# First stage of a two-block transformer kernel: which engine splits weights and doubles a rotation table

## The chip, the cores and the metric

The kernel runs on one core of a Trainium2 chip. The core has a matrix engine (TensorE, PE in the profile, whose weight loads are shown as PEld), two elementwise engines that this document is about, VectorE (DVE) and GpSimd (POOL), an engine for activation functions and copies (ScalarE, ACT), and SyncE (SP), which here only issues the loads. Each engine runs its own list of instructions strictly in order and waits on semaphores for the others. The metric is the device time of one execution in microseconds (us), lower is better. Three runs of the kernel before gave 973.45, 974.07 and 975.14 us, median 974.07.

## The reference

Two blocks run after each other on 256 tokens of width 1024, in float32. The part that matters here is the first half of the first block:

```
h = layer_norm(concat([meta (16 rows), x (256 rows)]))          # 272 x 1024
p = h @ w_in + b_in                                             # 1024 x 5640
u, q, k, v, o, i, f, g_s5, g_m = split(p)                       # widths 512 512 512 1024 1024 4 4 1024 1024
qk   = silu(causal_depthwise_conv(concat([q, k]), width 4))
s5   : x_t = exp(lambda*dt) x_{t-1} + Bbar u_t (complex);  y_t = Re(C x_t) + D u_t
mlstm: chunked matrix memory over q, k, v, i, f; head norm; times sigmoid(o)
mix  = sigmoid(g_s5) * glu(gelu(s5)) + sigmoid(g_m) * (mlstm @ m_w_out)
h    = layer_norm(alpha*h + mix @ w_o); then a feed-forward part; then the second block:
       attention, gated delta rule, mixture of experts, final norm
```

The complex recurrence of s5 is done as a real scan in a rotating frame: angle tables cos(n*theta) and sin(n*theta) for n = 0..63 turn the input into the frame and the state out of it.

## The kernel before

The float32 products are made of three fast ones: each operand is split into a rounded high part and a low remainder (`whi` and `wlo` for weights, `hTh` and `hTl` for the normalised tokens), and `ws` (L438) issues hi*hi, hi*lo and lo*hi. One slice of `w_in` is 128 columns wide: a 128x1024 tile, 24 matmuls of 272 (later 256) columns. The 45 slices are counted here as w0 to w44: w0 to w3 give u, w4 to w11 q and k, w12 the gates i and f, w13 to w20 v, w21 to w28 o, w29 to w44 the two mix gates.

For each slice `wsplit` (L417) lets ScalarE round the weights into `whi` and lets VectorE, or GpSimd if `eng` says so, subtract to get `wlo`. Both have three buffers, so the split of slice n waits until TensorE is through with slice n-3. `pool_turn` (L604) chose the engine: the first two slices in `ln0` (L594) and the next three (PT = 3) go to GpSimd, then from the 13th turn on every fourth, later every third: 14 of the 45, namely w0, w1, w3, w4, w5, w18, w22, w26, w30, w32, w35, w38, w41 and w44.

A q/k slice ends in one of two PSUM banks. ScalarE empties it into `pre` and `cv_y` (two buffers each), VectorE adds three shifted products to `cv_y` (`conv_silu`, L858), ScalarE takes a tanh (`cv_t`) and VectorE writes `qk`. So TensorE can be at most a few slices ahead of VectorE.

`s5_setup` (L634) makes the tables between these projections: a long run of small VectorE instructions (exponentials, angles, `bd`, `cz`), one Sin on ScalarE (`cs`), and then `double` (L728), six times: from the first 2^k columns of the two tables `rot` it makes the next 2^k by an angle addition of four products, a difference and a sum, each a tensor_tensor over 16 x 2^k elements a partition. 36 instructions in all, on GpSimd. The tables are first read after the v projection has begun, in `s5` (L742), which interleaves with v, o and gate projections: products with `rot` on VectorE, sums on GpSimd (`s5z`, 32 of them), scans on VectorE.

`block1` (L1007) calls these as generators in a fixed order. `ln0` runs in a hand-written order on VectorE, ScalarE and TensorE; from L1027 on a scheduler of the tile framework orders each engine's list from the order of emission and its own cost estimates, so that any edit can reorder the rest of the stage.

Of the kernel before, what the change touches and what calls it, by code (L numbers as in the profile page):

```python
# [11 lines left out]
OP = mybir.AluOpType  # L12
# [58 lines left out]
MS = {mybir.EngineType.DVE, mybir.EngineType.Activation, mybir.EngineType.PE}  # L71
NW0 = 1
NWU = 30
PT = 3
LT = 9
DCE = 1
QB = 3
# [1 line left out]
PV = 3  # L79
ORD0 = "0m1w"  # L80
PW = 4
P0 = 12
PP = [9]
L1A = [2, 2, 2, 2]
ORD = "abcdefmnopyz"
# [7 lines left out]
class K:  # L93
    def __init__(self, ctx, tc, a, out, dbg=None, stop=None):
# [3 lines left out]
        nc = self.nc  # L98
        self.V, self.S, self.G, self.PE, self.SP = nc.vector, nc.scalar, nc.gpsimd, nc.tensor, nc.sync
        self.const = self.pool("const", 1)  # L100
        self.DC = (self.G, self.V)[DCE]
        self.psx = None
# [118 lines left out]
    def setup(self):  # L221
        nc, a, const = self.nc, self.a, self.const
        V, G = self.V, self.G
        self.ones = const.tile([128, 128], F32, name="ones")
        jp = self.ones.bitcast(I32)
        G.iota(jp, pattern=[[1, 128]], base=0, channel_multiplier=-1)
        self.ident = const.tile([128, 128], F32, name="ident")
        self.ts(self.ident, jp, 0.0, OP.is_equal, eng=G)
        self.warm = const.tile([128, 1], F32, name="warm")

    def setup2(self, lp):
        nc, a, const = self.nc, self.a, self.const
        V, G = self.V, self.G
        jp = self.ones.bitcast(I32)
# [265 lines left out]
    def ln0(self):  # L500
# [27 lines left out]
        def chain(x, tag, dg, n=128):  # L528
            v, m, y, t = [lp.tile([128, 1], F32, name=f"r0{j}", tag=f"{tag}{j}")[:n] for j in range(4)]
            self.ts(v, x, 1.0, OP.mult, 1e-5, OP.add)  # L530
            self.ts(m, x, -0.5, OP.mult, -0.5e-5, OP.add)
            yield
            self.ts(y.bitcast(I32), v.bitcast(I32), -0.5, OP.mult, 1597463007.0, OP.add)
            yield
            for _ in range(3):
                self.stt(t, y, m, y, OP.mult, OP.mult)
                yield
                self.stt(y, t, 1.5, y, OP.add, OP.mult)
                yield
            self.ts(dg, self.ident[:n, :n], y, OP.mult)  # L540
            if n == 128:
                V.tensor_copy(self.rs0[:, int(tag[1]):int(tag[1]) + 1], y)

        def run(*gens):
            gens = list(gens)
            while gens:
                gens = [q for q in gens if next(q, 0) is None]

        def centre(x, h, ag):
            for cs in (slice(0, 512), slice(512, 1024)):  # L550
                self.stt(h[:, cs], x[:, cs], ag[:, 0:1], g[:, cs], OP.subtract, OP.mult)
                yield

        def stats(x, st, ag):
            for i in range(2):
                V.bn_stats(st[:, i], x[:, i * 512:(i + 1) * 512])
                yield
            V.bn_aggr(ag, st)
# [8 lines left out]
        def one(f):  # L567
            f()
            yield

        with self.tc.manual_schedule(engines=MS):
            for o, n in ((0, 32), (32, 4)):
                rs = slice(o, o + n)
                self.cpa(self.sel[rs], self.ident[rs, o:o + 4, None].to_broadcast([n, 4, 128]))
            brow = lp.tile([36, 256], F32R, name="brow0")
            self.act(brow, self.sel.bitcast(F32).rearrange("p a b -> p (a b)")[:, :256], AF.Copy, scale=0.0)
            p = self.ps("acc")
            for _ in range(NWU):
                self.tr(p[:, :128], self.ident)
            self.act(self.warm, self.ident[:, 0:1], AF.Tanh)  # L580
            self.act(brow[0:4], br.rearrange("p a b -> p (a b)"), AF.Copy)
            self.act(hs, xm, AF.Copy, accum_out=sm)
            run(stats(xs[0], st[0], ag[0]))
            run(one(lambda: self.tt(brow[32:36], br.rearrange("p a b -> p (a b)"), brow[0:4].bitcast(F32), OP.subtract)),
                chain(ag[0][:, 1:2], "l0", dg[0]), centre(xs[0], self.hres[0], ag[0]),
                self.late(3, one(lambda: self.ts(sm, sm, -1.0 / D, OP.mult))),
                self.late(4, stats(xs[1], st[1], ag[1])))
            self.act(hm, xm, AF.Identity, bias=sm)
            self.act(hs, hm, AF.Square, accum_out=qm)
            self.tt(hm, hm, g[:16], OP.mult, eng=self.G)  # L590
            tn = self.tn(16, self.hres[0], dg[0], self.hT, brow)
            run(chain(ag[1][:, 1:2], "l1", dg[1]), centre(xs[1], self.hres[1], ag[1]),
                one(lambda: self.ts(qm, qm, 1.0 / D, OP.mult)), self.late(3, chain(qm, "l2", dg[2], 16)), self.late(LT, tn))
            self.wsp = [self.wsplit(self.w0[0][:, :, j * 128:(j + 1) * 128], 0, eng=self.G) for j in range(2)]  # L594
            run(self.tn(144, self.hres[1], dg[1], self.hT, brow))
            next(ls)
            run(self.tn(0, hm, dg[2], self.hT, brow))
            self.setup2(lp)
            next(ls)
            wv = self.w0[1]  # L600
            self.wsp += [self.wsplit(wv[:, :, j * 128:(j + 1) * 128], 0) for j in range(NW0)]
        self.ls, self.sl = ls, sl

    def pool_turn(self):  # L604
        self.np += 1
        return self.G if self.np > P0 and self.np % (PW if self.np < PN else PV) == 0 or self.np <= PT else None

# [26 lines left out]
    def s5_setup(self, pool, tmp):  # L634
# [80 lines left out]
        tq = [tmp.tile([128, 16, 32], F32, name=f"tq{i}") for i in range(2)]  # L715
        self.G.memset(self.rot[0][:, :, 0:1], 1.0)
        self.G.memset(self.rot[1][:, :, 0:1], 0.0)
        for k in range(6):
            self.double(self.rot, k, 2 ** k, tq)
        yield  # L720
        for o, v in [(self.BT[i], bd[i].rearrange("p (c a) b -> p c (a b)", c=4)) for i in range(2)] + list(zip(self.CT, czs)):
            p = self.ps("acc")
            for c in range(4):
# [4 lines left out]
    def double(self, src, k, n, tq):  # L728
        C, Sn = src[0][:, :, 0:n], src[1][:, :, 0:n]
        cb = self.cs[:, 0, k, :][:, :, None].to_broadcast([128, 16, n])  # L730
        sb = self.cs[:, 1, k, :][:, :, None].to_broadcast([128, 16, n])
        oc, os_ = src[0][:, :, n:2 * n], src[1][:, :, n:2 * n]
        t0, t1 = tq[0][:, :, :n], tq[1][:, :, :n]
        G = self.G
        self.tt(oc, C, cb, OP.mult, eng=G)
        self.tt(t0, Sn, sb, OP.mult, eng=G)
        self.tt(oc, oc, t0, OP.subtract, eng=G)
        self.tt(os_, Sn, cb, OP.mult, eng=G)
        self.tt(t1, C, sb, OP.mult, eng=G)
        self.tt(os_, os_, t1, OP.add, eng=G)  # L740

    def s5(self, pool):  # L742
        Z, tail, Q = {}, {}, {}
# [603 lines left out]
    def gdn(self, pool, hp):  # L1347
# [36 lines left out]
        self.tt(v4(AD), v4(AT), bc(self.bm32), OP.mult, eng=(None, self.G)[PA])  # L1384
        PT = dT
        self.tt(PT, pq, dT, OP.mult)
        yield
# [120 lines left out]
        for j in range(4):  # L1508
            self.mm(po[:, TS[j]], PT[:, TS[j]], z[:, TS[j]], True, True)
        for e in range(2):  # L1510
# [34 lines left out]
    def moba(self, pool, mx, c):  # L1545
# [3 lines left out]
        for t in range(2):  # L1549
# [10 lines left out]
            yield  # L1560
        PT = []
        for s in range(2):
# [7 lines left out]
        for s in range(2):  # L1570
            pT = self.ps("acc")
            for i in range(3):
                self.tr(pT[:, i * 128:(i + 1) * 128], P[s][:, i * 128:(i + 1) * 128])
            PT.append(pool.tile([128, SHW], F32, name="mo_PT", tag="g_sq", bufs=2))
            self.cp(PT[s], pT[:, :384])
# [594 lines left out]
```

## Time and profile before

One execution was profiled: it took 974.35 us, 0.28 us over the median of the three runs; its span from first to last instruction is 972.6 us.

| | busy us | share of the span | instructions |
|---|---|---|---|
| PE | 901.6 | 93% | 6208 |
| DVE | 605.0 | 62% | 1414 |
| ACT | 408.5 | 42% | 798 |
| POOL | 143.4 | 15% | 145 |

The mean granted clock of TensorE is 0.944 of full speed. Of POOL's 143.4 us, 121.9 us fall into the first 300 us. The first stage, up to the end of the `w_in` projections, lasts to about 262 us. A row of a timeline reads: start, duration, engine, source line, operation, what it writes <- what it reads, shape, count of merged instructions; in brackets the idle time of that engine just before it and who ended it. L139 is the helper through which every tensor_tensor goes, so that names of tiles tell the work apart.

### The profile page before, as it was taken

How to read it: one execution, taken by the hardware profiler on the slowest of the kernel's cores; microseconds unless marked ns; L12 is line 12 of the kernel's file. 1: busy time of each engine (PE TensorE's matmuls, PEld its weight loads, DVE VectorE, ACT ScalarE, POOL GpSimd, SP SyncE). 2: the span in 40 equal slices, each digit the busy share in tenths (PEclk: the TensorE clock that was granted, in tenths of full speed). 3: DMA queues.
4: the chain of work that ended last, by engine and by line, in shares of the span. 5: the costliest groups of instructions: out<-in, count | busy, mean ns of one | idle time of the engine just before them, and what ended most of it. 6: DMA issues, size and time to landing. Idle time of an engine off the chain costs nothing. (4 is left out here: it accounts for less than half of the span.)

```text
span 972.6 us, 15977 instructions
## 1 busy us (share of the span) xinstructions
PE 901.6 (93%) x6208; PEld 680.1 (70%) x6208; DVE 605.0 (62%) x1414; ACT 408.5 (42%) x798; POOL 143.4 (15%) x145
## 2 busy tenths in 40 slices
PE   8977988989879999999999899999999999999983
PEld 6967766778879899998887898786654334444421
DVE  6698699776778757665567788667463222232213
ACT  4355224364746326564552266476441112222102
POOL 5293243223640000000000010100030000000001
PEclk7898789789999999999999999999969999999996
DMA  7524222124457636565774544424967999999971
GB/s 182 163 82 138 79 87 87 44 87 130 155 200 232 216 130 173 174 185 178 243 262 130 172 132 131 130 88 154 385 240 260 365 396 407 404 406 408 406 256 47
DMA packets 111172, 198.09 MB, mean 204 GB/s; under 512 B 13177, under 2 KB 77922, under 8 KB 111090
## 3 DMA queue, kind: packets, MB, share of 16 engines
q1 hardware_dynamic: 110802, 196.47, 58.4%
q8 instruction: 51, 0.84, 0.4%
q10 hardware_dynamic: 288, 0.52, 0.1%
q14 instruction: 31, 0.25, 0.1%
HBM read 195.93 MB, written 1.05 MB: 203 GB/s over the span
## 5 line engine op out<-in xcount | busy, mean ns | idle before, releaser
L139 DVE TENSOR_TENSOR wlo<-w,whi 128x1024 fp32r<-128x1024 f32 x137 | 173.8, 1271 | 85.7 <-ACT whi L154 85.2
L154 ACT ACTIVATE whi<-w 128x1024 fp32r<-128x1024 f32 x151 | 159.0, 1057 | 161.9 <-PE ps_mm L132 98.5
L132 PE MATMUL ps_mm<-hTh,whi 128*128 128x256 f32 (+1 forms) x360 | 110.8, 308 | 16.0 <-ACT cv_y L151 11.1
L132 PE MATMUL ps_mm<-hph,whi 128*128 128x256 f32 x424 | 122.1, 288 | 0.0
L132 PE MATMUL ps_mm<-hph,wlo 128*128 128x256 f32 x424 | 120.9, 285 | 0.0
L132 PE MATMUL ps_mm<-hpl,whi 128*128 128x256 f32 x424 | 120.4, 284 | 0.0
L132 PE MATMUL ps_acc<-w,xg 128*64 128x512 f32 x512 | 118.2, 599 | 0.0
L132 PE MATMUL ps_mm<-hTh,wlo 128*128 128x256 f32 (+1 forms) x360 | 108.8, 302 | 1.7 <-DVE wlo L139 1.0
L132 PE MATMUL ps_mm<-hTl,whi 128*128 128x256 f32 (+1 forms) x360 | 108.6, 302 | 0.0
L132 PEld LDWEIGHTS ps_mm<-hTh,whi 128*128 128x128 f32 x360 | 74.4, 207 | 20.9 <-ACT cv_y L151 11.8
L132 PEld LDWEIGHTS ps_acc<-w,xg 128*64 128x64 f32 x512 | 35.6, 137 | 68.6 <-issue 64.3
L132 PEld LDWEIGHTS ps_mm<-hph,whi 128*128 128x128 f32 x424 | 79.9, 189 | 1.8 <-issue 1.8
L132 PEld LDWEIGHTS ps_mm<-hph,wlo 128*128 128x128 f32 x424 | 79.9, 188 | 1.2 <-issue 1.2
L132 PEld LDWEIGHTS ps_mm<-hpl,whi 128*128 128x128 f32 x424 | 79.9, 188 | 0.6 <-issue 0.6
L132 PEld LDWEIGHTS ps_mm<-hTh,wlo 128*128 128x128 f32 x360 | 74.1, 206 | 2.1 <-DVE wlo L139 1.1
L132 PEld LDWEIGHTS ps_mm<-hTl,whi 128*128 128x128 f32 x360 | 74.3, 206 | 1.7 <-issue 1.7
L132 PE MATMUL ps_acc<-w,mhT 128*32 128x512 f32 x512 | 61.1, 608 | 1.0 <-DVE mhT L1994 1.0
L139 DVE TENSOR_TENSOR hpl<-ps_acc,hph 128x512 fp32r<-128x512 f32 x40 | 26.0, 686 | 52.8 <-ACT hph L154 52.8
L148 DVE SCALAR_TENSOR_TENSOR mth<-mth,ps_acc 128x256 f32<-128x256 f32 x16 | 6.7, 420 | 82.5 <-ACT mth L151 82.5
L151 ACT ACTIVATE mth<-ps_acc,cb 128x256 f32<-128x256 f32 x16 | 7.6, 474 | 119.9 <-PE ps_acc L132 119.9
L154 ACT ACTIVATE hph<-ps_acc 128x512 fp32r<-128x512 f32 (+1 forms) x44 | 23.6, 576 | 65.8 <-PE ps_acc L132 64.9
L139 POOL TENSOR_TENSOR wlo<-w,whi 128x1024 fp32r<-128x1024 f32 x14 | 36.0, 2580 | 81.0 <-ACT whi L154 69.7
(600 smaller groups left out, 1839.1 us busy)
## 6 DMA issues: line engine op xcount, KB each, us to landing
w<-in_w_down_dram SPq DMA_DIRECT2D x46, 1024.0 KB, 6.1
w<-in_w_in_dram SPq DMA_DIRECT2D x36, 1024.0 KB, 5.4
w<-in_w_gate_dram SPq DMA_DIRECT2D x60, 512.0 KB, 8.3
w<-in_w_up_dram SPq DMA_DIRECT2D x60, 512.0 KB, 11.0
w<-in_w_up_dram SPq DMA_DIRECT2D x16, 1024.0 KB, 6.8
w<-in_m_w_out_dram SPq DMA_DIRECT2D x4, 1024.0 KB, 6.4
w<-in_s_w_glu_dram SPq DMA_DIRECT2D x8, 512.0 KB, 4.7
w<-in_w_o_dram SPq DMA_DIRECT2D x4, 1024.0 KB
```

What stands on the lines that cost most here:

```text
L132: self.PE.matmul(out, lhsT, rhs, start=start, stop=stop, **kw)
L139: (eng or self.V).tensor_tensor(out, a, b, op)
L148: (eng or self.V).scalar_tensor_tensor(out, a, s, b, op0, op1, **kw)
L151: self.S.activation(out, in_, func, bias=bias, scale=scale, **kw)
L154: self.S.activation(out, in_, AF.Copy)
```

## The change

Three things change. `PT = 0` and `P0 = 1000` make `pool_turn` return None every time, and the two splits of `ln0` lose their `eng`: all 45 subtractions for `wlo` run on VectorE. `double` runs on VectorE too, with its four products ahead of the difference and the sum. And the `yield` of `s5_setup` moves from behind the six doublings to ahead of them: they are emitted at the generator's second call, which `block1` makes in its loop over the four q/k blocks of 256 columns at i == 3 (QB = 3), between the sixth and the seventh q/k slice as emitted, together with the transposes of `bd` and `cz` that stood there already.

```
-PT = 3
+PT = 0
-P0 = 12
+P0 = 1000
@@ ln0
-            self.wsp = [self.wsplit(self.w0[0][:, :, j * 128:(j + 1) * 128], 0, eng=self.G) for j in range(2)]
+            self.wsp = [self.wsplit(self.w0[0][:, :, j * 128:(j + 1) * 128], 0) for j in range(2)]
@@ s5_setup
         self.G.memset(self.rot[1][:, :, 0:1], 0.0)
+        yield
         for k in range(6):
             self.double(self.rot, k, 2 ** k, tq)
-        yield
@@ double
-        G = self.G
-        self.tt(oc, C, cb, OP.mult, eng=G)
-        self.tt(t0, Sn, sb, OP.mult, eng=G)
-        self.tt(oc, oc, t0, OP.subtract, eng=G)
-        self.tt(os_, Sn, cb, OP.mult, eng=G)
-        self.tt(t1, C, sb, OP.mult, eng=G)
-        self.tt(os_, os_, t1, OP.add, eng=G)
+        self.tt(oc, C, cb, OP.mult)
+        self.tt(t0, Sn, sb, OP.mult)
+        self.tt(os_, Sn, cb, OP.mult)
+        self.tt(t1, C, sb, OP.mult)
+        self.tt(oc, oc, t0, OP.subtract)
+        self.tt(os_, os_, t1, OP.add)
```

Three places of the new order matter. The first is VectorE in the small instructions of `s5_setup`, where `ex_q` is a polynomial's running value. Before:

```order
L139 TENSOR_TENSOR wgr<-wgr,FB 128x288
L148 SCALAR_TENSOR_TENSOR ex_q<-ex_q,ex_f 128x16 x3
L148 SCALAR_TENSOR_TENSOR ex_y<-ex_q,ex_e 128x16
L139 TENSOR_TENSOR rl<-FC,ex_y 128x16
L139 TENSOR_TENSOR th<-FC,ex_y 128x16
```

After:

```order
L139 TENSOR_TENSOR wlo<-w,whi 128x1024
L148 SCALAR_TENSOR_TENSOR ex_q<-ex_q,ex_f 128x16
L139 TENSOR_TENSOR wlo<-w,whi 128x1024
L148 SCALAR_TENSOR_TENSOR ex_q<-ex_q,ex_f 128x16
L866 MEMSET pre 128x3 x2
L148 SCALAR_TENSOR_TENSOR ex_q<-ex_q,ex_f 128x16
L139 TENSOR_TENSOR wgr<-wgr,FB 128x288
L148 SCALAR_TENSOR_TENSOR ex_q<-ex_q,ex_f 128x16
```

The two splits that came in are those of w4 and w5; w3's stands a little earlier, behind w2's.

The second place is VectorE behind the split of w11, the last q/k slice. Before, convolution steps (`cv_y`, `qk`) stand between that split and the one of w12:

```order
L139 TENSOR_TENSOR wlo<-w,whi 128x1024
L148 SCALAR_TENSOR_TENSOR qk<-cv_t,cv_y 128x272 x2
L867 MEMSET pre 128x3
L148 SCALAR_TENSOR_TENSOR cv_y<-pre,FA,cv_y 128x272 x2
L139 TENSOR_TENSOR wlo<-w,whi 128x1024
```

After, 25 of the 36 instructions of the doubling stand there without anything between them; these are the last of them, then the split of w12 and what follows:

```order
L139 TENSOR_TENSOR rot_553<-rot_553,cs 128x16x32
L139 TENSOR_TENSOR tq_565<-rot_554,cs 128x512
L139 TENSOR_TENSOR rot_554<-rot_554,cs 128x16x32
L139 TENSOR_TENSOR tq_566<-rot_553,cs 128x512
L139 TENSOR_TENSOR rot_553<-rot_553,tq_565 128x16x32
L139 TENSOR_TENSOR rot_554<-rot_554,tq_566 128x16x32
L139 TENSOR_TENSOR wlo<-w,whi 128x1024
L866 MEMSET pre 128x3 x2
L139 TENSOR_TENSOR wlo<-w,whi 128x1024
L148 SCALAR_TENSOR_TENSOR cv_y<-pre,FA,cv_y 128x272 x6
```

This block stands behind all convolution steps of w4 to w9 (the other 11 instructions of the doubling stand among those) and ahead of those of w10 and w11. Ahead of the split of w12 there are 18 `cv_y` and 6 `qk` rows after, 14 and 4 before.

The third place is VectorE ahead of the first state products of s5, `s5q` (the rows at L808 and L807 are the scans). Before:

```order
L139 TENSOR_TENSOR s5t<-ps_acc,rot_554 128x512
L808 SCALAR_TENSOR_TENSOR s5z<-s5decay,s5z 128x256 x2
L139 TENSOR_TENSOR s5c<-s5zm,s5carry 128x8 x2
L139 TENSOR_TENSOR s5q<-s5z,rot_553 128x2x4x64 x2
L139 TENSOR_TENSOR s5z<-s5z,rot_554 128x2x4x64 x2
```

After:

```order
L139 TENSOR_TENSOR s5t<-ps_acc,rot_554 128x512
L807 SCALAR_TENSOR_TENSOR s5z<-s5decay,s5z 128x256 x2
L139 TENSOR_TENSOR wlo<-w,whi 128x1024
L139 TENSOR_TENSOR s5q<-s5z,rot_553 128x2x4x64 x2
L139 TENSOR_TENSOR s5z<-s5z,rot_554 128x2x4x64 x2
```

A split that GpSimd made came into this run of instructions, on which the output product of s5 on TensorE waits. GpSimd's own list in the stage keeps the constants, the product for the meta rows, four copies and the 32 sums `s5z`.

## Rows read from the trace of the kernel before

**Rows 1.** Stretches of the stage: us, busy time and count per engine, granted clock, DMA.
```profile
35.00:80.00 45.00, 31.54 (x221) 29.96 (x221) 43.91 (x122) 22.59 (x36) 35.43 (x45) 0.91 0.31 94
...
140.00:200.00 60.00, 54.83 (x329) 40.65 (x330) 54.42 (x126) 22.74 (x56) 16.76 (x14) 0.87 0.22 69
```

**Rows 2.** Timeline of PE: four matmuls that waited, with idle time and releaser.
```profile
78.30 0.59 PE L132 MATMUL ps_mm<-hTh,whi 128*128 128x272 f32 x1 [7.28 <-ACT cv_y L151]
...
137.95 1.57 PE L132 MATMUL ps_acc<-s5q,CT 128*32 128x256 f32 x4 [3.40 <-DVE s5q L139]
...
169.87 0.70 PE L132 MATMUL ps_acc<-vt,mwm 16*128 16x257 f32 x2 [3.47 <-DVE mwm L148]
...
245.03 0.39 PE L132 MATMUL ps_mm<-hTh,whi 128*128 128x256 f32 x1 [3.25 <-ACT gth L151]
```

**Rows 3.** Timeline of POOL: two splits, then the first and last doubling rows (36 instructions).
```profile
40.49 4.73 POOL L139 TENSOR_TENSOR wlo<-w,whi 128x1024 fp32r<-128x1024 f32 x2 [4.82 <-ACT whi L154]
49.55 1.25 POOL L139 TENSOR_TENSOR rot<-rot,cs 128x16 f32<-128x16 f32 x1 [4.32 <-ACT cs L151]
...
74.66 1.34 POOL L139 TENSOR_TENSOR rot<-rot,tq 128x512 f32<-128x512 f32 x1
```

**Rows 4.** Timeline of DVE in the q/k part, beside and after GpSimd's work.
```profile
35.32 0.22 DVE L322 COPY FB<-ps_mm 128x57 f32<-128x57 f32 x1 [5.82 <-PE ps_mm L136]
...
40.40 4.86 DVE L148 SCALAR_TENSOR_TENSOR ex_q<-ex_q,ex_f 128x16 f32<-128x16 f32 x3
...
57.13 1.32 DVE L139 TENSOR_TENSOR wlo<-w,whi 128x1024 fp32r<-128x1024 f32 x1
...
68.87 4.80 DVE L148 SCALAR_TENSOR_TENSOR cv_y<-pre,FA,cv_y 128x272 f32<-128x272 f32 x4
...
77.00 0.98 DVE L148 SCALAR_TENSOR_TENSOR qk<-cv_t,cv_y 128x272 f32<-128x272 f32 x2
...
79.23 1.25 DVE L139 TENSOR_TENSOR wlo<-w,whi 128x1024 fp32r<-128x1024 f32 x1
...
88.62 0.43 DVE L148 SCALAR_TENSOR_TENSOR qk<-cv_t,cv_y 128x272 f32<-128x272 f32 x1
88.97 1.57 DVE L148 SCALAR_TENSOR_TENSOR cv_y<-pre,FA,cv_y 128x272 f32<-128x272 f32 x3
```

**Rows 5.** Timeline of DVE: rows of three sizes, for the price of a doubling.
```profile
51.56 0.38 DVE L139 TENSOR_TENSOR cw<-cw,FC 128x16 f32<-128x16 f32 x3
...
53.33 0.41 DVE L139 TENSOR_TENSOR Bq<-B,cw 128x256 f32<-128x256 f32 x1
...
139.53 1.28 DVE L139 TENSOR_TENSOR s5q<-s5z,rot 128x512 f32<-128x512 f32 x2
```

**Rows 6.** Timeline of ACT: two roundings that waited for TensorE to free a buffer.
```profile
83.36 1.06 ACT L154 ACTIVATE whi<-w 128x1024 fp32r<-128x1024 f32 x1 [2.00 <-PE ps_mm L132]
...
89.41 1.06 ACT L154 ACTIVATE whi<-w 128x1024 fp32r<-128x1024 f32 x1 [0.80 <-PE ps_mm L132]
```

**Rows 7.** Groups of POOL's instructions up to 262 us: count | busy us, mean ns | idle.
```profile
L139 POOL TENSOR_TENSOR wlo<-w,whi 128x1024 fp32r<-128x1024 f32 x14 | 36.0, 2580 | 81.0 <-ACT whi L154 69.7 <-ACT mst L151 11.2
L139 POOL TENSOR_TENSOR s5z<-s5z,s5t 128x256 f32<-128x256 f32 x32 | 27.9, 898 | 64.6 <-DVE s5t L139 56.6 <-DVE s5z L139 8.0
```

**Rows 8.** Timeline of DVE in the s5 part: a free pair of scans, then five rows beside a split on POOL.
```profile
128.64 1.27 DVE L808 TENSOR_TENSOR_SCAN s5z<-s5decay,s5z 128x256 f32<-128x256 f32 x2
...
132.69 3.36 DVE L808 TENSOR_TENSOR_SCAN s5z<-s5decay,s5z 128x256 f32<-128x256 f32 x2
...
161.21 3.81 DVE L139 TENSOR_TENSOR s5q<-s5z,rot 128x512 f32<-128x512 f32 x2
...
193.61 2.87 DVE L139 TENSOR_TENSOR s5q<-s5z,rot 128x512 f32<-128x512 f32 x1
...
207.57 2.04 DVE L139 TENSOR_TENSOR mve<-mc 128x8 f32<-128x8 f32 x1
...
232.86 2.62 DVE L139 TENSOR_TENSOR s5z<-s5z,s5c 128x8 f32<-128x8 f32 x3 [1.75 <-POOL s5z L139]
```

## The prediction

> **What bounds the kernel now.** I read the stretches of the stage first, then TensorE's waits, then the timelines of the engines that end them. The change touches only the first 262 us. What follows is a chain of TensorE work whose weight loads are freed by TensorE itself, so that what TensorE gains or loses in the first stage should reach the end one to one.
>
> In the q/k part, 35 to 80 us, VectorE is busy 43.91 of 45 us and TensorE 31.54; from 140 to 200 it is 54.42 of 60 against 54.83 [rows 1]. So VectorE sets the pace in the q/k part, and in the s5 part the two alternate. TensorE's longest waits say the same: 7.28 us at 78.30 for a PSUM bank that ScalarE empties late because VectorE's convolutions are late, and 3.40, 3.47 and 3.25 us in the s5 part, each behind a VectorE chain [rows 2]. After the 7.28 us TensorE also starts slowly: slice w10 takes 5.0 us, from 78.30 to 83.3, where ScalarE gets the buffer back, while w11 and w12 take 6.05 together [rows 2, 6]; the granted clock of the stretch, 0.91, says that it was not at full speed throughout [rows 1].
>
> What the reader is to see next is that much of VectorE's busy time is no work. While GpSimd runs the two splits of w4 and w5 from 40.49 to 45.22, three VectorE instructions on 16 elements take 4.86 us [rows 3, 4]; three of that size take 0.38 elsewhere [rows 5]. While GpSimd doubles the table, 49.55 to 76.00 [rows 3], four convolution steps take 4.80 us, against 1.57 for three when GpSimd is idle [rows 4]. In the s5 part five rows stand beside a GpSimd split and are two to ten times as long as their like [rows 8]. The two engines hold each other up when both read tensors, and the waiting shows as busy.
>
> **The change, part by part: q/k.** A ledger of VectorE from 35.3, where it starts after 5.82 us of idle, to the end of w12's split at 80.5: 45.2 us [rows 4].
>
> Stalls that go: 4.86 - 0.4 = 4.5 at the splits of w4 and w5. From 57.13 to 78.0 stand five splits, eleven cv_y and four qk (first and last in [rows 4]); at 1.2, 0.5 and 0.35 (a row starts before the last one ends: qk at 88.62, the next at 88.97) they are 6.0 + 5.5 + 1.4 = 12.9 and took 20.8, so 7.9 are lost. What remains as work is 45.2 - 4.5 - 7.9 = 32.8.
>
> What comes in ahead of w12's split: the splits of w4 and w5, 2.4; four more cv_y and two more qk by the new order, 2.7; and the doubling. (w0's and w1's splits fall into the tail of the norm and w3's into the idle 5.82 us, at no cost; if that idle were gone, 1.2 each.) The trace has no doubling on VectorE. Rows of 16, 256 and 512 elements take 0.13, 0.41 and 0.64 [rows 5]; a straight line through them gives 0.13, 0.15, 0.18, 0.25, 0.38 and 0.64 for the six sizes, times six 10.4, and about 9.5 with the overlap of neighbours. The bounds: 6 x 1008 elements at the rate of the 512-element row alone, 7.6, and GpSimd's own 26.4 for the same 36 [rows 3]. I take 9.5, from the same engine.
>
> Sum: 35.3 + 32.8 + 2.4 + 2.7 + 9.5 = 82.7 for the end of w12's split. That is later than the 80.5 of before, but TensorE is two slices further: w10 and w11 no longer wait for the doubling, since the convolutions of w8 and w9, which free their banks, stand ahead of it. What is late next is w12 itself. TensorE can issue two of its 24 matmuls, then waits some 7 us for this block of doubling, and starts as slowly as w10 did: 22/24 of w10's 5.0 us, so w12 ends at 82.7 + 4.6 = 87.3. Before, it ended at 89.4, when ScalarE gets the buffer for w15 [rows 6]. The gain is 2.1. Queued behind the doubling on VectorE are w13's split (0.1 later, before TensorE needs it) and the convolutions of w10 and w11; nobody needs their qk until the s5 and matrix-memory part. SP's list of loads keeps its order; each load starts when its buffer comes free.
>
> **The s5 part.** Nine splits, w18 to w44, go from GpSimd (2.58 each in the mean of the 14 [rows 7]) to VectorE (1.2 each): 10.8. Read against the stalls they end, in the order in which the new list places them:
> the scans at 132.69 lose 3.36 - 1.27 = 2.1 and one split comes in, net 0.9;
> s5q at 161.21 loses 3.81 - 1.28 = 2.5, one comes in, and GpSimd's sums, which stood around its split, now stand together, for which I keep 0.4: net 0.9;
> s5q at 193.61 loses 2.87 - 0.64 = 2.2 and two come in: 0;
> mve at 207.57 loses 1.9, one comes in: 0.7;
> s5z at 232.86 loses 2.2, one comes in: 1.0 [rows 5, 8].
> The other three go where VectorE waits for ScalarE's rounding anyway (w18's behind the gate chain); were it busy there, 1.2 each. Together 3.5 of 10.9, all on chains for which TensorE waits, so less than the waits themselves [rows 2].
>
> **Sum.** 2.1 + 3.5 = 5.6. The profiled execution took 974.35, its span 972.6 and 1.75 around it; 974.35 - 5.6 = 968.75, and as it lies 0.28 above the median of the runs, 968.5.
>
> The Trainium skill has a rule that speaks against this: Perfetto Trace Analysis, section Optimizing Scalar/DVE Operations, says that when VectorE is saturated, giving work to ScalarE or even to GpSimd may make sense. By that rule alone, taking 11.9 us (2.4 + 9.5) back in the full q/k part would make it 986. The same section warns that the two share a read port, so that moving work between them may not help; the 4.86 us row sides with the warning [rows 4].
>
> **Rivals.**
> Slower: VectorE becomes the bound of the s5 part. The 32 sums s5z, 898 ns each [rows 7], stay on GpSimd; whatever VectorE instruction moves up into the place of a vanished stall may meet them instead, so that the stall only changes its victim. For it: three of the five stalled rows stand next to such sums, and VectorE is at 90% [rows 1]. Against: rows beside sums alone lose little. The price: of the six splits on the chains, 7.2, all show; with 2 of the 10.9 recovered and 2.1 from q/k, that is 974.07 + 7.2 - 2 - 2.1 = 977.2. It decides once less than about 3 of the 10.9 come back.
>
> Flat: the doubling on VectorE costs 12 or more, since each of its sums waits for a product just ahead of it. Every us above 9.5 delays w12 by one; at 12 the q/k gain is gone, and with half of 3.5 the time is 972.3. For it: 25 instructions stand there without anything else to fill a wait. Against: two others stand between each product and its sum.
>
> Larger: shorter waits also let the granted clock stay up (0.91 and 0.87 [rows 1]). Of the four waits in [rows 2], 17.4 us, about 4.9 are counted above; if half of the other 12.5 go as well, 962.3. For it: the engines feed each other in turn, so one chain's gain starts the next earlier. Against: w12's wait replaces the longest.
>
> That the splits and the doubling do not move at all is excluded: the new lists have none on GpSimd.
>
> **How the numbers follow.** The forecast, 965.5 to 971.5, gets 0.47; the larger gain 0.18; flat, 971.5 to 976, 0.22; slower 0.13 (0.02 of it for the rule's 986). A difference of 0.2%, 1.95 us, is about what a measurement of this kernel can tell from none. Below 972.1 lie the first two and a third of the flat case: 0.72. Within 0.2%: 0.15. Slower: 0.13. The range, 960 to 978, holds the centres of both outer cases and ends a little beyond them.
>
> **What would show it.** In the new profile: ex_q as short as its neighbours at 40 us; splits and convolution steps between 45 and 75 at 1.2 and 0.5; the doubling's 36 rows at 9 to 10 us in all; TensorE's longest wait in the q/k part no longer before w10 but inside w12, 6 to 8 us, ending at 81 to 84; w12 through at 87; scans and s5q pairs at 1.3. The prediction is wrong if VectorE's rows stay long with GpSimd idle, if the doubling takes over 12, if TensorE's waits after 100 us grow, or if something after 262 us gives the gain back: a wait of TensorE for a weight load there would show that.

## The result, and the profile after

| | runs | median us | range |
|---|---|---|---|
| before | 4 | 973.76 | 972.49 to 975.14 |
| after | 4 | 955.92 | 955.13 to 959.46 |

The ratio is 0.982, with an interval of 0.9802 to 0.9837: 17.5 us faster. The forecast was 5.6 us, its range ended at 960, and the direction was right. The profiled execution of after took 955.7 us, its span is 953.9. One execution of w3_one, an experiment below (1687.8 us), and one of before (1233.82) lie far above all others of their kernel and are left out of the medians and ratios below.

The stretches of after, with the columns of [rows 1] (duration, busy us and count of PE, PEld, DVE, ACT and POOL, granted clock, DMA share, GB/s):

```profile
35.00:80.00 45.00, 35.02 (x259) 33.95 (x259) 42.56 (x162) 26.11 (x43) 1.53 (x4) 0.93 0.33 103
140.00:200.00 60.00, 57.43 (x388) 43.73 (x381) 55.14 (x152) 31.83 (x76) 7.49 (x8) 1.00 0.28 88
```

GpSimd is nearly gone from the first stretch and halved in the second, VectorE is as busy as before in both, and TensorE is busier. The granted clock from 140 to 200 us is 1.00 instead of 0.87.

TensorE's waits, which answer to [rows 2] (start, duration, operation, in brackets the idle time before it and who ended it):

```profile
79.70 0.60 PE L132 MATMUL ps_mm<-hTh,wlo 128*128 128x272 f32 x1 [5.95 <-DVE pre L866]
130.98 1.57 PE L132 MATMUL ps_acc<-s5q,CT 128*32 128x256 f32 x4 [2.41 <-DVE s5q L139]
161.85 0.70 PE L132 MATMUL ps_acc<-vt,mwm 16*128 16x257 f32 x2 [1.10 <-DVE mwm L148]
223.61 0.38 PE L132 MATMUL ps_mm<-hTh,whi 128*128 128x256 f32 x1 [0.41 <-ACT gth L151]
```

The first is the wait inside w12 that takes the place of the one before w10. The other three are the same places as the last three of [rows 2]. VectorE and ScalarE in the q/k part of after, for [rows 3, 4 and 6]: the polynomial, the start and the end of the block of 25 doubling rows, the two splits behind it, and the rounding that waits for w12:

```profile
45.17 0.17 DVE L148 SCALAR_TENSOR_TENSOR ex_q<-ex_q,ex_f 128x16 f32<-128x16 f32 x1
...
70.67 0.20 DVE L139 TENSOR_TENSOR rot<-rot,tq 128x32 f32<-128x32 f32 x1
...
77.23 1.28 DVE L139 TENSOR_TENSOR rot<-rot,tq 128x512 f32<-128x512 f32 x2
78.43 2.37 DVE L139 TENSOR_TENSOR wlo<-w,whi 128x1024 fp32r<-128x1024 f32 x2
...
84.38 1.06 ACT L154 ACTIVATE whi<-w 128x1024 fp32r<-128x1024 f32 x1 [0.64 <-PE ps_mm L132]
```

How far after is ahead, read at the same matmul in both timelines of TensorE:

| matmul | before | after | ahead by |
|---|---|---|---|
| transpose of `fb_rows`, ahead of w2 | 35.01 | 33.66 | 1.35 |
| transpose of `ifr`, behind w12 | 90.94 | 85.91 | 5.03 |
| first `s5q,CT` | 137.95 | 130.98 | 6.97 |
| the `vt,mwm` that waited 3.47 us before | 169.87 | 161.85 | 8.02 |
| first `ident,qk` transpose | 213.11 | 197.35 | 15.76 |
| first `ymh,whi`, end of the stage | 266.63 | 243.77 | 22.86 |
| first `glh,whi`, in the mix | 298.12 | 277.64 | 20.48 |
| last `hph,whi` | 666.40 | 646.27 | 20.13 |
| end of the span | 972.6 | 953.9 | 18.7 |

So up to the end of w12 after gained 3.7 us, where 2.1 was forecast (1.35 of the 5.03 stand ahead of w2), in the rest of the stage 17.8 us instead of 3.5, and some 4 us were given back after 266 us.

### The profile page after: what moved, and what is told of

Its sections match the earlier page's. It is cut to its first block, busy times and chain, and to the rows that moved or that the text cites. A ratio compares the mean times of both kernels' runs of the same rounds, so it can differ in the third digit from the quotient of the medians.

```text
span 953.9 us, 15976 instructions
## 1 busy us (share of the span) xinstructions
PE 894.3 (94%) x6208; PEld 673.3 (71%) x6208; DVE 598.2 (63%) x1463; ACT 409.8 (43%) x799; POOL 82.8 (9%) x95
## 4 chain that ended last, share of the span: by engine, by line
PE 72%; DVE 17%; ACT 5%; issue 2%; DMA 2%; POOL 1%; SPq 0%; DVEq 0%; ACTq 0%; POOLq 0%
PE ps_acc L132 41%; PE ps_mm L132 24%; PE ps_wo L132 5%; DVE wlo L139 4%; PE ps_acc L136 3%; ACT whi L154 2%; DVE cv_y L148 1%; DVE s5z L807 1%; POOL w L139 1%; DMA gain<-in_ln_b_dram 1%; DVE s5z L139 1%; DVE w L148 1%; DMA w<-in_m_w_out_dram 1%; DVE r L148 1%; ACT mo_P L151 1%
## 5 line engine op out<-in xcount | busy, mean ns | idle before, releaser
L139 DVE TENSOR_TENSOR wlo<-w,whi 128x1024 fp32r<-128x1024 f32 x151 | 190.1, 1262 | 87.6 <-ACT whi L154 87.0
L132 PE MATMUL ps_mm<-hTh,wlo 128*128 128x256 f32 (+1 forms) x360 | 105.7, 294 | 7.6 <-DVE pre L866 6.0
L132 PE MATMUL ps_mm<-hTh,whi 128*128 128x256 f32 (+1 forms) x360 | 107.5, 299 | 0.9 <-ACT gth L151 0.4
L132 PE MATMUL ps_mm<-hTl,whi 128*128 128x256 f32 (+1 forms) x360 | 104.9, 292 | 0.0
L132 PEld LDWEIGHTS ps_mm<-hTh,wlo 128*128 128x128 f32 x360 | 70.7, 196 | 8.9 <-DVE pre L866 6.2
L132 PEld LDWEIGHTS ps_mm<-hTh,whi 128*128 128x128 f32 x360 | 70.8, 197 | 6.2 <-issue 2.7
L132 PEld LDWEIGHTS ps_mm<-hTl,whi 128*128 128x128 f32 x360 | 70.6, 196 | 0.8 <-issue 0.7
L132 PEld LDWEIGHTS ps_acc<-w,mhT 128*32 128x32 f32 x512 | 20.0, 112 | 35.6 <-issue 31.2
```

Source lines behind the costliest of these rows:

```text
L132: self.PE.matmul(out, lhsT, rhs, start=start, stop=stop, **kw)
L139: (eng or self.V).tensor_tensor(out, a, b, op)
```

## Experiments

All ratios are to the kernel before, run beside it on the same chip. Where the text gives a gain in us, it is one minus the ratio, times 974.

### Which part of the change

**x1_late**: before, with `P0 = 1000` only.

> The kernel before with only the nine late splits (w18 to w44) on VectorE; the early splits and the doubling stay on GpSimd at their old place. Theory A (each stall sits on a chain for which TensorE waits, and each wait is followed by matmuls at the lower clock, so a wait costs about twice its length): the s5 part gains most of the 16.8 us that it gained in the whole change, TensorE's waits at 169.9, 198.5, 213.1 and 245.0 shrink to under 1.2 us each and the granted clock from 140 to 262 us is 1.00: 959 to 964 us. Theory B (the forecast's pricing, net 3.5 us): 970.5. Theory C (the s5 part gained because it began earlier, or because both halves of the change are needed): within 2 us of before, 972 to 975.

Measured: 962.95 us, ratio 0.9882 (0.9868 to 0.9895), 11.5 us faster. **x2_front**: after, with `P0 = 12`.

> The changed kernel with the nine late splits back on GpSimd (P0 = 12): early splits and doubling as changed. Theory A: only the gain up to the end of w12, 5 to 6 us, is left, and the s5 part waits as before: 967.5 to 969. Theory B (the forecast): 972 (2.1 less than before). Theory C (an earlier start carries through the s5 part): 960 or less.

Measured: 970.7 us, ratio 0.9963 (0.9947 to 0.9978), 3.6 us faster. **x3_double**: as x2_front, and `PT = 3` and the `eng=self.G` of the two splits in `ln0` as before.

> The kernel before with only the doubling changed: on VectorE, products first, emitted behind the fourth pair of projections; all 14 splits as before. Stalls of 7.9 us go, 9.5 us of work come in, and the convolutions of w8 and w9 come ahead of it. Theory A: TensorE's wait before w10 (7.28 us) goes and one of some 6 us inside w12 comes; w12 ends 0 to 2 us earlier than before: 972 to 974. The forecast by its own ledger: 4.5 us of stalls stay and 2.4 us of splits stay away, so the end of w12's split is 84.8 and w12 through at 89.4: 974.

Measured: 972.62 us, ratio 0.9981 (0.9971 to 0.9992), 1.9 us. **x4_early**: before, with `PT = 0` and without the two `eng=self.G` in `ln0`.

> The kernel before with only the five early splits (w0, w1, w3, w4, w5) on VectorE; the doubling stays on GpSimd at its old place and the late splits too. Theory A: the start is some 1 us earlier already before 35 us, and 4.5 us of stalls go against 2.4 us of splits: 3 us at w12, 970 to 971.5, if the convolutions behind the doubling do not eat it. The forecast by its own ledger: 2.1 us, 972. A rival (GpSimd's doubling sets the pace up to 76 us whatever stands ahead of it, and starts no earlier): 973 to 974.

Measured: 972.38 us, ratio 0.9984 (0.9971 to 0.9997), 1.6 us. Two thirds of the gain are the nine late splits alone; with x2_front's 3.6 they make 15.1 of the 17.5, and the intervals cover the difference. Theory C fell with x1_late and x2_front, and Theory B, the forecast's price, with x1_late; x2_front came out a little slower than Theory A said. The early splits and the doubling give 1.6 (the ledger's 972 was right there) and 1.9 (a little more than its 974), and together 3.6. TensorE's waits in x1_late at the places of [rows 2]:

```profile
136.31 1.13 PE L132 MATMUL ps_acc<-s5q,CT 128*32 128x256 f32 x4 [2.34 <-DVE s5q L139]
167.63 0.70 PE L132 MATMUL ps_acc<-vt,mwm 16*128 16x257 f32 x2 [1.10 <-DVE mwm L148]
206.51 0.33 PE L136 MATMUL ps_acc<-ident,qk 128*128 128x128 f32 x1 [0.26 <-ACT qk L151]
230.81 0.39 PE L132 MATMUL ps_mm<-hTh,whi 128*128 128x256 f32 x1 [0.41 <-ACT gth L151]
```

They are close to those of after, although nothing of the q/k part was changed. The granted clock from 140 to 262 us is 0.97 here, against 0.90 before; Theory A had said 1.00.

### Is it GpSimd's reading, and what does one stall cost

The new lists could have gained by their order. **y3_shadow** leaves the order of after untouched on every other engine and adds the reading alone (code shortened; `scr` is a scratch tile):

```
-            self.tt(lo, wv, hi.bitcast(F32), OP.subtract, eng=eng)
+            self.tt(lo, wv, hi.bitcast(F32), OP.subtract)
+            if eng is not None:     # the nine late turns, P0 = 12
+                self.tt(scr, wv, hi.bitcast(F32), OP.subtract, eng=eng)
```

> The changed kernel, and at the nine late turns GpSimd makes the same subtraction once more into a scratch tile that nobody reads; the lists of the other engines stay as in the changed kernel. Theory A (GpSimd reading two tensors stalls VectorE, and the stalls on the chains were the price of the late splits): the stalls and TensorE's waits come back, on top of VectorE's own nine splits: 967 to 975. Rival (the s5 part gained by the new order of its lists, or by wlo being ready earlier, not by the missing stalls): 955 to 958.

Measured: 976.53 us, ratio 1.0026 (1.001 to 1.0041): all 17.5 us are gone and 2.5 more, just beyond Theory A's range. GpSimd, two pairs of VectorE and one wait of TensorE in y3_shadow:

```profile
160.08 3.36 POOL L139 TENSOR_TENSOR scr<-w,whi 128x1024 f32<-128x1024 f32 x1
...
161.12 4.01 DVE L139 TENSOR_TENSOR s5q<-s5z,rot 128x512 f32<-128x512 f32 x2
...
168.87 1.22 PE L132 MATMUL ps_acc<-vt,mwm 16*128 16x257 f32 x2 [3.53 <-DVE mwm L148]
...
198.68 4.86 DVE L139 TENSOR_TENSOR s5z<-s5z,rot 128x512 f32<-128x512 f32 x2
```

A subtraction that nobody reads turns a pair that takes 1.28 alone [rows 5] into 4.0 to 4.9. **w2_onein** replaces it by an instruction with one input tensor, `self.ts(scr, hi.bitcast(F32), 1.0, OP.mult, eng=eng)`.

> As y3_shadow, but the nine extra instructions on GpSimd read one tensor (whi times 1.0 into the scratch tile) instead of two. If it is the reading of two tensors on both engines that stalls VectorE: no VectorE row beside them is longer than its like, 955 to 959 (the sums s5z stand behind them on GpSimd and may come a little late). If any work of GpSimd in the memory stalls VectorE: 965 to 976, as y3_shadow.

Measured: 956.97 us, ratio 0.9821 (0.9803 to 0.984), as in after; the profiled execution is the slowest of five, 962.16. GpSimd and VectorE in w2_onein at the same place, then at w41's turn, and last the pair of w41's turn in after, where GpSimd is idle:

```profile
156.31 3.74 POOL L143 TENSOR_SCALAR scr<-whi 128x1024 f32<-128x1024 f32 x1
...
157.35 2.12 DVE L139 TENSOR_TENSOR s5q<-s5z,rot 128x512 f32<-128x512 f32 x2
```

```profile
231.36 3.82 POOL L143 TENSOR_SCALAR scr<-whi 128x1024 f32<-128x1024 f32 x1 [8.96 <-ACT whi L154]
...
232.46 2.13 DVE L139 TENSOR_TENSOR s5q<-s5z,rot 128x512 f32<-128x512 f32 x2
```

```profile
226.33 1.29 DVE L139 TENSOR_TENSOR s5q<-s5z,rot 128x512 f32<-128x512 f32 x2
```

Here GpSimd takes longer (2.78 at its shortest, 3.74 and 3.82 here), and VectorE is held up as well, but less: such a pair takes 2.1 beside the instruction with one input, 1.29 alone and 4.0 beside the subtraction. The expectation that no row would be longer than its like did not hold. At the place of the first pair after itself has 2.35, beside the sums. In w2_onein no row of VectorE lost more than 0.85 us beside a shadow; the stalled rows of y3_shadow lost 1.0 to 3.6. TensorE's wait for `mwm`, 1.10 in after, is 1.64 in w2_onein and 3.53 in y3_shadow. So it is above all GpSimd instructions that read two tensors that stop VectorE; those with one input do so briefly, and a cost of that in time is not shown. GpSimd's sums have a shadow ahead of them in both kernels, so a late sum is not what y3_shadow lost by. The two shadows differ in the operation too (a product with a number, a difference); that was not tested apart.

**w3_one** keeps a single shadow, at w26's turn (`self.np == 24`).

> The changed kernel with one extra subtraction on GpSimd instead of nine, at w26's turn, where it meets the s5q pair behind which the second mwm and TensorE wait. The price of a single stall of 2 to 3 us on such a chain. If the wait alone counts: TensorE's wait at 162 us goes from 1.10 to 3.5 us, and the time up by 2.4: 958.3. If each wait is followed by matmuls at the lower clock, as behind the wait at 169.87 before: 3.5 from the wait and up to 5 more from the clock, 961 to 964.

Measured: 961.4 us, ratio 0.9869 (0.9849 to 0.989) against 0.982 of after, 4.8 us more. The wait, and two stretches around it in w3_one; below them the same stretches of after:

```profile
162.75 1.03 PE L132 MATMUL ps_acc<-vt,mwm 16*128 16x257 f32 x2 [3.51 <-DVE mwm L148]
```

```profile
147.00:163.00 16.00, 12.49 (x81) 9.75 (x80) 15.97 (x33) 8.10 (x18) 7.03 (x5) 1.00 0.22 67
163.00:175.00 12.00, 12.00 (x43) 7.87 (x42) 7.18 (x16) 1.73 (x5) 3.25 (x4) 0.57 0.29 87
```

```profile
147.00:163.00 16.00, 14.90 (x92) 11.12 (x90) 15.93 (x38) 8.16 (x19) 4.25 (x4) 1.00 0.21 67
163.00:175.00 12.00, 11.07 (x68) 8.22 (x67) 10.30 (x27) 4.05 (x12) 3.25 (x4) 1.00 0.27 87
```

The wait grew from 1.10 to 3.51, by 2.4 us, and the 12 us behind it ran at a granted clock of 0.57, most of them at the lower level of 1.2 GHz, with 43 matmuls instead of 68. Between the `vt,mwm` at 147.58 and the one at 188.40 in after, w3_one goes from 1.5 ahead to 4.4 behind, 5.9 us. The same stretch, first in after, then in w3_one:

```profile
147.58:188.40 40.82, 38.66 (x257) 28.88 (x256) 39.05 (x102) 19.20 (x48) 7.49 (x8) 1.00 0.24 78
```

```profile
146.07:192.79 46.72, 43.21 (x257) 31.71 (x256) 41.73 (x102) 19.19 (x48) 10.28 (x9) 0.89 0.22 68
```

The same 257 matmuls are busy 4.5 us longer; the rest is the longer wait, less a wait of 0.93 at 174.31 that only after has. The expectation with the clock in it, 961 to 964, held (0.9869 of 974 is 961); the one without it, 958.3, lies just outside the interval (959.3 to 963.3).

### Where the doubling stands

**y1_oldplace**: after, with the `yield` of `s5_setup` back behind the six doublings, all else as after.

> The changed kernel with the doubling, on VectorE, back at its old place ahead of the yield. Theory A: the same 9.5 us of VectorE work, only earlier: TensorE's wait of 5.95 us inside w12 goes and waits of about the same sum come ahead of w7 to w11: 954 to 958. Forecast's reason for the new place (it lets the convolutions of w8 and w9 free their banks ahead of the doubling): 958 to 961.

Measured: 954.94 us, ratio 0.9791 (0.9769 to 0.9814). **y2_poolnew**: after, with `eng=self.G` in the six instructions of `double`.

> The changed kernel with the 36 instructions of the doubling on GpSimd, emitted at the new place, products first. VectorE loses 9.5 us of work and meets up to 26 us of GpSimd's reading instead. Theory A: the stalls of 7.9 us come back at about the size of the work taken away, a part of them later, on the gate chain behind w12: 955 to 960. Rival (what counts is VectorE's work ahead of w12's split): 950 to 953.

Measured: 958.23 us, ratio 0.9834 (0.9813 to 0.9855). Both intervals overlap that of after. In y1_oldplace one wait of 8.53 us stands at 68.11 in place of the 5.95 at 79.70; in y2_poolnew they are 4.30 at 71.69 and 3.23 at 82.73. With the splits on VectorE, neither the place of the doubling nor its engine could be told apart by time: the work moves the wait.

### What gives back after 266 us

In the mix, SP's queue holds a load of a bias into `gain1` ahead of the fourth load of `m_w_out`. SP in after:

```profile
241.69 0.57 SPq L326 DMA_DIRECT2D gain<-in_ln_b_dram  x1
...
258.83 0.34 SPq L326 DMA_DIRECT2D gain<-in_ln_b_dram  x1
259.27 0.38 SPq L414 DMA_DIRECT2D w<-in_m_w_out_dram  x1
```

The load at 258.83 waited 9.2 us for GpSimd's four additions of the first bias, which read the buffer, and the weights stood behind it. TensorE waited for them at 269.48 (3.96). Its wait of 1.91 at 260.93 has another cause: z1_noload has it too, 1.95 at 261.95. In the path that runs here nothing reads the second bias. **z1_noload**: after, with `g, b = self.gain(pool, "ln1_g", "gain0"), None`.

> The changed kernel without the second load of a norm's bias into gain1 in the mix part, which nothing reads there. Before and after, that load stands on SP's queue ahead of the fourth load of m_w_out and waits there until GpSimd is through with four products; TensorE then waits 1.91 and 3.96 us for the weights. Theory D (this queue gives back some 2 us of what the first stage gains, and the wait can go): the load starts up to 4 us earlier, the two waits shrink by 2 to 4 us and the clock stays higher: 951 to 954. Rival (the buffer of the ring is free only then, or the transfer is slowed by others): 955 to 957.

Measured: 949.9 us, ratio 0.9748 (0.9725 to 0.9771), 6 us less than after by the medians, 7 by the ratios. SP in z1_noload, and the stretch behind the stage in after and in z1_noload:

```profile
254.24 0.39 SPq L414 DMA_DIRECT2D w<-in_m_w_out_dram  x1
```

```profile
262.00:300.00 38.00, 34.04 (x255) 33.87 (x255) 28.27 (x43) 20.31 (x29) 0.00 (x0) 0.88 0.76 252
```

```profile
262.00:300.00 38.00, 38.00 (x293) 36.78 (x294) 34.82 (x54) 23.62 (x34) 0.00 (x0) 1.00 0.78 251
```

The load starts 5 us earlier, the wait of 3.96 is gone, and the clock stays at 1.00. The range of 951 to 954 was again too timid, by the clock.

### How far the lesson goes

Four kernels on top of z1_noload. **v1_hres**: the eight residual instructions of the mix on VectorE (without `eng=self.G`).

> z1_noload with the eight instructions on the residual in the mix part (scale by rs0m, add of the bias, 128x512 each), which GpSimd makes from 240 to 259 us, on VectorE. In the changed kernel three splits and one tm stand beside them at 2.0 to 2.3 us instead of 1.2, and TensorE waits 1.95 us behind them at 261. Theory A (two readers stall each other): VectorE loses some 4 us of stalls and takes 5 us of work, a part of it into its idle time; TensorE's wait of 1.95 us shrinks: 947 to 950.5. Rival (the adds wait for their load and hold VectorE's list): 951 to 954.

Measured: 954.68 us, ratio 0.9793 (0.9774 to 0.9812), 4.4 us slower than z1_noload. VectorE in v1_hres, and the matmul that waited for it:

```profile
253.82 1.29 DVE L139 TENSOR_TENSOR w<-w,gain 128x512 f32<-128x512 f32 x2 [2.47 <-DMA gain<-in_ln_b_dram]
```

```profile
256.71 0.58 PE L132 MATMUL ps_mm<-yml,whi 128*128 128x256 f32 x1 [3.16 <-DVE yml L139]
```

The rival was right: the adds wait for their load, and `yml`, which TensorE needs, stands behind them. **v2_sums**: the 32 sums `s5z` on VectorE (`t, self.V` for `t, G` in `elem`).

> z1_noload with the 32 sums s5z on VectorE too, so that GpSimd does nothing in the s5 part. Theory A carried too far would say faster: the last stalls (a split of 1.57 and an s5q pair of 2.35 at 155 to 158 us) and the waits of 1.75 us for the sums go, 945 to 949. The count of work says slower: 32 sums of 256 elements at 0.41 are 13 us on an engine that is busy 55 of 60 us from 140 to 200, against some 2 us of stalls and 5 us of waits: 953 to 958. I hold the second likelier.

Measured: 943.28 us, ratio 0.968 (0.966 to 0.9699), faster by 6.6. My likelier case was wrong. The same stretch of the s5 part as above, in v2_sums:

```profile
140.00:200.00 60.00, 59.15 (x400) 46.85 (x393) 54.19 (x152) 30.75 (x70) 0.00 (x0) 0.94 0.31 93
```

VectorE's busy time in it did not grow (54.19, in after 55.14), and TensorE's rose from 57.43 to 59.15. From the transposes of `mr` to the first `ymh`, the same work in both, VectorE was busy 127.9 us in z1_noload and 130.8 in v2_sums, for sums that are 12.2 us of work: the other 9 us were waiting that had shown as busy. **v3_later**: the second `next(ss)` and what closes behind it, after the q/k loop.

> z1_noload with the doubling and the transposes behind it emitted after the last q/k projection instead of before it; 12 of its 36 instructions then fall in between convolutions of w8 to w10, the rest behind w11's convolutions. Theory A (only what stands ahead of a split counts): TensorE's wait of 5.95 us inside w12 shrinks to 0 to 3 us, unless the first state projections now wait for the tables: 945 to 949. Rival (VectorE is saturated to 80 us whatever the order, so the wait only moves): 949 to 951.

Measured: 952.51 us, ratio 0.9779 (0.976 to 0.9798), 3 us slower, though its interval overlaps that of z1_noload (0.9725 to 0.9771). w12 came 6.3 us earlier (`ifr` at 80.26, in z1_noload 86.53), but the gate chain, which stands behind the doubling now, came 3.3 us later (`mr` at 101.00, 97.73), with waits of TensorE of 3.60 us for a split at 87.53 and of 2.42 for `lf` at 98.22. **v4_oldplace**: the `yield` behind the doublings.

> z1_noload with the doubling on VectorE at its old place, ahead of the yield. From y1_oldplace against the changed kernel (954.9 against 955.9, within the spread): 948 to 950, the same as z1_noload.

Measured: 946.14 us, ratio 0.9721 (0.9699 to 0.9743), a little below the expectation; its interval overlaps that of z1_noload. Both times, here and in y1_oldplace, the old place of the doubling came out ahead, by 2.6 and 2.8 us; neither comparison alone is clear of the spread. **w1_both**: z1_noload, v2_sums and v4_oldplace together.

> The changed kernel without the unused load, with the 32 sums s5z on VectorE and the doubling at its old place (z1_noload, v2_sums and v4_oldplace together): GpSimd does nothing from the setup to the mix part. If the gains add (949.9 - 3 - 6): 938 to 943. If both remove the same waits: 943 to 946.

Measured: 939.81 us, ratio 0.9657 (0.9639 to 0.9676): 33 us less than before, nearly twice the gain of the change, and the fastest kernel here. The same stretch in it:

```profile
140.00:200.00 60.00, 58.37 (x413) 47.35 (x413) 56.50 (x161) 35.30 (x78) 0.00 (x0) 1.00 0.38 115
```

## Why the prediction was right, and where it was wrong

**The q/k part: the mechanism right, the gain too small.** `ex_q` is 0.17 long, the 25 doubling rows take 7.76 (70.67 to 78.43) and the other 11 about 1.2, so 9.0 where 9.5 was forecast from [rows 5]. The wait moved into w12, 5.95 us (6 to 8 forecast), and ended at 79.7 (81 to 84 forecast). w12's split ended at 79.6 and not 82.7: 1.35 of it is the earlier start told next, the other 1.7 are work that the ledger counted too high (0.5 in the doubling, the rest in the 32.8). Of the 5.0 us by which after was ahead behind w12, 1.35 were there ahead of w2, and not by the change: y3_shadow, z1_noload and x2_front have the same lists there and reach that transpose at 35.26, 35.38 and 34.68. That part is luck of the profiled execution. The front part alone, x2_front, gave 3.6 (2.1 to 5.2), against 2.1 forecast.

**The s5 part: the mis-sized term.** The step was "net gains" of 0.9, 0.9, 0, 0.7 and 1.0, together 3.5: each stall less the splits that come in. It named the right mechanism, five rows that did stall (`mve`, 2.04 against 0.17, twelve times its like and not ten) and the chains behind them; x1_late measured 11.5. What TensorE waited for at the end of each chain, in before and in after:

| chain | wait before | after | net forecast |
|---|---|---|---|
| scans, then `s5q` | 3.40 + 0.74 | 2.41 + 0.75 | 0.9 |
| `s5q`, then `mwm` | 3.47 | 1.10 + 0.93 | 0.9 |
| `s5q`, then `gth` | 1.28 | 0 | 0 |
| `mve`, then `qk` | 2.32 + 0.26 | 0.26 | 0.7 |
| `s5z`, then `gth` | 3.25 | 0.41 | 1.0 |

Two errors stand in it. The first is in the waits: they shrank by 8.9 us, 14.7 to 5.9, where 3.5 was counted. The splits do stand on these chains, as charged (the one at 154.82 ahead of the `s5q` pair at 156.31, those at 215.41 and 218.67 ahead of the last `gth`). But more left the chains than the five stalls. The `s5z` pair beside GpSimd's sums on the way to `mwm` went from 2.35 (at 164.93) to 1.28 (at 158.59). By the new order one `s5q` row of 0.6 stands behind `mwm` now, and two scans with their small rows, 1.9, behind the `gel_t` that ScalarE needs ahead of the last `gth`. And w18's split, counted at nothing, had stalled a sixth row on a chain to TensorE, the scan `mr`, behind which TensorE waited 1.72 us before and 0.74 in after (not in the table). The scan in before, then in after:

```profile
101.38 1.70 DVE L924 TENSOR_TENSOR_SCAN mr<-lfr,ifr 4x272 f32<-4x272 f32 x1
```

```profile
96.34 0.71 DVE L923 TENSOR_TENSOR_SCAN mr<-lfr,ifr 4x272 f32<-4x272 f32 x1
```

The second error is the clock, which the forecast priced at nothing. From the first `vt,mwm` to the first `ymh` the stage took 112.9 us before and 96.2 in after, first and second below:

```profile
153.70:266.63 112.93, 102.01 (x721) 86.03 (x721) 88.46 (x189) 56.73 (x111) 40.87 (x29) 0.91 0.31 97
```

```profile
147.58:243.77 96.19, 92.96 (x720) 77.91 (x720) 84.73 (x197) 56.77 (x111) 24.04 (x22) 1.00 0.36 113
```

The waits in it explain 7.9 of the 16.7; the other 9 are busy time of the same matmuls at a granted clock of 0.91 instead of 1.00. In before the slow matmuls stand behind the waits: the clock is 0.50 to 0.66 from 170 to 182 us and 0.57 from 246 to 250. A shorter wait did not always bring this back: behind its wait of 2.41 the changed kernel, too, ran at 0.50 (134 to 138 us), and between `mr` and the first `vt,mwm`, where this wait stands, nothing was gained (50.6 us before, 50.5 in after). w3_one shows it for a single wait. The rival "larger" said just this; it was given 0.18, and its 962.3 still lay 6.4 us above the result.

**The slower rival** named a real thing, the sums that stay on GpSimd and meet whatever moves up: a split of 1.57 and an `s5q` pair of 2.35 beside them at 154 to 158 us. These two lost 1.4 us, a scan pair of 1.75 and a split of 1.68 at 126.88 and 128.55 about 0.9 more. It did not come to the 7.2 of the rival, and TensorE's waits did not grow; but that rows beside sums alone lose little was a wrong reading, and v2_sums shows that these stalls, too, were worth removing. **The flat rival** fell with the doubling's 9.0 us.

**The rule's 986** was off by 30 us. Perfetto Trace Analysis of the Trainium skill, section Optimizing Scalar/DVE Operations, says that a saturated VectorE may give work away, even to GpSimd, which speaks for leaving the splits on GpSimd; x1_late and v2_sums took work back onto the busy engine and were faster. The warning in the same section, that moving work between these two might not help, is what held.

**One to one after 262 us** was wrong as an assumption and right as a test: the text named a wait for a weight load as what would show it. That wait stands in before as well, 4.31 us at 290.91 against 3.96 in after, so that the change did not make it. From the first `ymh` to the first `glh` after takes 2.4 us longer (33.87 against 31.49), and 2.1 of that is busy time of the same matmuls (27.72 against 25.62) at a granted clock of 0.85 instead of 0.95. x1_late lost 2.7 of 15.7 and x2_front 2.0 of 6.0 in the same stretch, there mostly by longer waits; z1_noload takes 26.37. Where the further 1.4 us between 646 us and the end went, no run was made for.

## What to carry to other kernels

A busy engine may be busy waiting: when VectorE rows on which TensorE waits are long only beside GpSimd instructions that read two tensors, move those back, even if VectorE looks full, and count what stands ahead of the instruction that TensorE needs, not the sum of the work. Off such a chain it brought nothing here: the doubling cost the same on either engine (y2_poolnew), and the additions of v1_hres made VectorE wait for their load. Price a wait of TensorE at its length plus the slow stretch that may follow it; here 2.4 us cost 4.8. Before crediting a gain to the end, look at what stands in front of the next weight load on its queue: a load that nobody reads cost 6 us.

## What was not expected

GpSimd with one input tensor held VectorE up by at most 0.85 us at a meeting (w2_onein, nine instructions, no loss of time to be seen), GpSimd with two for most of the rest of the GpSimd instruction (y3_shadow, 20 us). The Trainium skill, SBUF — State Buffer, section Who interferes with whom, says that a VectorE instruction with two inputs in SBUF contends with a GpSimd instruction that reads SBUF; the runs here agree, and show that the loss is much smaller where GpSimd reads one tensor. Where VectorE had only one of its inputs in SBUF, nothing was lost, as that section says: of the products from PSUM in the group below, about half overlap GpSimd's sums, and all take 0.67 to 0.69. None of them stands beside a shadow; the `mw` row at 197.88 in y3_shadow, which reads PSUM too, does, and takes 0.55 as elsewhere. The group in after and in y3_shadow:

```profile
L139 DVE TENSOR_TENSOR s5z<-ps_acc,rot 128x512 f32<-128x512 f32 x16 | 10.9, 679 | 3.2 <-PE ps_acc L132 3.1
```

```profile
L139 DVE TENSOR_TENSOR s5z<-ps_acc,rot 128x512 f32<-128x512 f32 x16 | 10.9, 682 | 4.7 <-PE ps_acc L132 4.7
```

The clock behind a wait of about 1 us is not the same in each execution. v1_hres and z1_noload have the same lists up to the end of the stage, and in both TensorE waits 0.94 us near 175 us; in v1_hres the six microseconds from 178 us ran at half the clock (in x1_late, too, it was 0.58 from 182 to 186 us, behind a wait of 0.92):

```profile
178.00:184.00 6.00, 6.00 (x43) 3.07 (x42) 4.28 (x17) 0.66 (x3) 0.00 (x0) 0.54 0.00 0
```

```profile
178.00:184.00 6.00, 6.00 (x64) 4.65 (x56) 6.00 (x20) 2.79 (x5) 0.00 (x0) 1.00 0.01 1
```

That one difference is worth 3 us, as much as the spread of the runs of one kernel; a single profile can be off by that.
